# Down projection: the last six depth tiles move from plain products to seven-product quads in two token groups, with weights issued ahead of operands

## The chip, the cores and the metric

The kernel runs on one core of one Trainium2 chip. The metric is the time of one execution on the device in microseconds (us); for the kernel before it is the median of three runs. A profile of one further execution was taken and is what all rows below come from. Engines are named as the profile names them: PE (TensorE matmul), PEld (TensorE weight load), DVE (VectorE), ACT (ScalarE), POOL (GpSimd), SP (SyncE, whose queue, SPq, issues all transfers of this kernel).

## The reference, cut to what matters

One layer of a decoder step over 2048 prompt tokens and 64 sample tokens, width 1024:

```python
h = rms_norm(x, pre_mix_g)
z = h @ w_in                        # q, k, v, sg_u, sg_v, mq, gate_logits (3 x 1024)
attn = windowed_attention(q, k, v)  # 8 heads of 64
sg   = spatial_gating(gelu(sg_u), layer_norm(gelu(sg_v)))
memo = memory_attention(mq, mem_k, mem_v)
proj = einsum('blnc,ncd->blnd', stack([attn, sg, memo]), w_o)
mixed = sum(sigmoid(gate_logits) * proj, axis=branch)
x = x + rms_norm(mixed, post_mix_g)
up = rms_norm(x, pre_ffn_g) @ w_up               # 1024 -> 2 x 2816
gate, val = split(conv3(up) + conv_b)            # width-3 causal convolution
f = (gelu_tanh(gate) * val) @ w_down             # 2816 -> 1024
y = x + rms_norm(f, post_ffn_g)
```

The outputs are y, the new window keys and values, the memory keys and values, the normalised spatial-gating values of the samples and the last rows of `up`.

## The kernel before

All 2112 tokens are laid out with channels on the 128 partitions and tokens on the free axis. Products are done in float32 split into a high and a low part (`split`: ACT rounds to the high part, line 76, then DVE subtracts, line 77), and each product of 128 channels takes three matmuls (`PASSES`: high-high, high-low, low-high).

The work runs in these stages. `pass_a`: projections and both attentions. `pass_b`: spatial gating. `gate_phase`: the 3 x 1024 gate logits and their sigmoid. `mix_phase`: output projection, gating, sum, post norm. `up_phase`: the up projection with convolution and gelu, writing `act_d` to DRAM. `down_phase`: the down projection and the final norm.

From `gate_phase` on the tokens are taken in three groups of 704 (`T2`), each in two chunks of 352 (`CW`). Gate, up and most of down use a seven-product scheme (class `Strassen`): a block of two output tiles by two chunks, over eight depth tiles of 128 (two halves of `HK` = 4), takes seven products of 4 x 3 = 12 matmuls of 128x352, 84 instead of 96. The products need seven weight operands (three raw ones, `a11`, `a12`, `a22`, and four sums, `s1` to `s4`) and seven token operands (`b11`, `t1`, `b21`, `t2`, `b22`, `t3`, `t4`, each of four tiles). `operands` loads the tokens, forms differences on DVE (line 793) and splits each tile (28 splits, 16 differences). `weights` loads the raw parts (line 824) and splits them, and loads the sums ready made and already split from `sum_d` in DRAM (line 850). Each of the seven weight operands takes one tile of the pool `wo`, which has ten tiles in up and down.

The sums for up and down are made earlier by `prep_sums`: one call loads four blocks of 256 KB (line 108), forms four sums on DVE (line 113), splits each, and stores four tiles of 512 KB to `sum_d` (line 116). The calls for the 22 up tiles stand in `pass_b` (the first `NF1` = 14, two behind each of the first seven of nine token items) and in the gate jobs of groups 1 and 2 (eight); eight calls for down stand between jobs of `up_phase`, two in group 0, five in group 1, one in group 2. In `pass_b` they have a pool of two weight tiles and one of five raw tiles; the pools of `gate_phase` lie over these.

`down_phase` has, in each group, two blocks `b` of eight depth tiles, each four `quad`s of seven products (line 885 by way of `product`), whose results are added into eight sum tiles `ys` (lines 1235 on ACT and 1240 on DVE). The six remaining depth tiles (`ND`) go through `plain`: eight output tiles by two chunks, each 6 x 3 = 18 matmuls (line 1285), with operands from `load_acts`, an addition into `ys` (line 1293) and the squares for the final norm (lines 1295 to 1299). `load_acts` takes its tiles from the pools of `b22`, `t3` and `t4`. `final` (lines 1302 to 1320) scales and adds the residual and stores; for groups 0 and 1 it is written behind the first quad of the next group. The pool of sum tiles, `yd`, has ten.

The order on each engine is laid down when the kernel is built, by a planner with times of its own that takes what is ready by the order of the program text; `high_priority` moves a piece ahead. An engine runs its list in that order and waits at the head of it. In `jobs`, `operands` of a group stands ahead of `weights` of its first job.

In `mix_phase`, `post_mix` of one group runs among the matmuls of the next: for each of eight tiles DVE scales `m` in place (line 1004), POOL adds `x` in place (line 1007), the result is stored and squared. `ffn_phase` makes the pools of up and down; `up_phase` begins with `ops0`, the token operands of group 0, under `high_priority(None)`.

Of the kernel before, what the change touches and what calls it, by code (L numbers as in the profile page):

```python
# [15 lines left out]
P = 128  # L16
# [7 lines left out]
T2 = 704  # L24
# [10 lines left out]
NF1 = 14  # L35
# [8 lines left out]
def tile_decoder_layer(ctx, tc, I, O):  # L44
# [9 lines left out]
    sum_d = [dpool.tile([4, P, 2, 512], F32, tag=f"sumd{f}", name=f"sum_d{f}") for f in range(NF + 20)]  # L54
# [48 lines left out]
    def prep_sums(rw, wo, w, sums, nm):  # L103


        def block(i):
            t = rw.tile([P, 512], F32, tag="raw", name=f"r{i}_{nm}")
            nc.sync.dma_start(out=t, in_=w[:, i * 512 : (i + 1) * 512])
            return t

        def total(i, p, m, op):
            t = rw.tile([P, 512], F32, tag="raw", name=f"s{i}_{nm}")
            nc.vector.tensor_tensor(out=t, in0=p, in1=m, op=op)
            r = wo.tile([P, 2, 512], F32R, tag="w", name=f"ws{i}_{nm}")
            split(r[:, 0], r[:, 1], t)
            nc.sync.dma_start(out=sums[i], in_=_f(r))
# [632 lines left out]
def stage2(tc, I, O, br, rbc_d, x1_d, acx_d, act_d, sum_d, sg_d, gains, split, PASSES, rstd_rows, prep_sums, m_d, acm_d):  # L749
# [14 lines left out]
    class Strassen:  # L764
# [9 lines left out]
        def operands(self, xs, nm, gain, rb):  # L774
# [21 lines left out]
            J = range(HK)  # L796
# [6 lines left out]
            for j in J:  # L803
                load(j + HK)
                put("b21", j, chunk(x[j + HK], 0))
            for j in J:
                put("t2", j, sub(t[j], chunk(x[j + HK], 1), t[j]))
            for j in J:
                put("b22", j, chunk(x[j + HK], 1))
            for j in J:  # L810
                put("t3", j, sub(chunk(x[j], 1), chunk(x[j + HK], 1), chunk(x[j], 1)))
            for j in J:
                put("t4", j, sub(t[j], chunk(x[j + HK], 0), t[j]))
            return ops

        def weights(self, w, sums, first, nm):

            _, _, wo, rw, _, _ = self.pools
            raw = {}

            def block(i):
                if i not in raw:
                    raw[i] = rw.tile([P, HK * P], F32, tag="raw", name=f"r{i}_{nm}")
                    nc.sync.dma_start(out=raw[i], in_=w[:, i * 512 : (i + 1) * 512])
# [17 lines left out]
            for n, i in (("a11", 0), ("s1", 0), ("a12", 1), ("s2", 2), ("s4", 3), ("s3", 1), ("a22", 3)):  # L842
                t = wo.tile([P, 2, HK * P], F32R, tag="w", name=f"w{n}_{nm}")
                if n[0] == "a":
                    split(t[:, 0], t[:, 1], block(i))
                elif first:
                    split(t[:, 0], t[:, 1], total(i))
                    nc.sync.dma_start(out=sums[i], in_=_f(t))
                else:
                    nc.sync.dma_start(out=_f(t), in_=sums[i])  # L850
# [25 lines left out]
        def product(self, q, bank, w, o, start):  # L876
# [5 lines left out]
            ps, n = banks[bank], 0  # L882
            for j in range(HK):
                for a, b in PASSES:
                    nc.tensor.matmul(  # L885
                        ps[:, :CW], lhsT=ws[w][:, a, j], rhs=ops[o][j][:, b],
                        start=(start and n == 0), stop=(n == 3 * HK - 1), skip_group_check=True,
# [19 lines left out]
def gate_phase(c2, tc, env):  # L907
# [572 lines left out]
```

## Time and profile before

| | |
|---|---|
| time, median of 3 runs | 2978.36 us (2975.37 to 2981.42) |
| profiled execution, its own time | 2972.76 us |
| its span, first to last instruction | 2970.9 us |
| granted TensorE clock, mean | 0.984 |
| PE busy | 2868.4 us, 97% |
| DVE, ACT, POOL busy | 69%, 47%, 17% |
| HBM traffic over the span | 246 GB/s |

The span is 1.9 us short of the profiled execution's time, and that time is 5.6 us short of the median. In the tables of stretches the figures behind the length are the busy time of each engine in it, in the order PE, PEld, DVE, ACT, POOL, each with its count of instructions, then the granted clock (1.00 is 2.4 GHz), the share in which the DMA engines were busy, and GB/s. In the timelines a row is a start, a length, and what ran; in brackets stands the idle time ahead of it and what ended it. Neighbouring matmuls and vector instructions overlap a little in these rows, so a rate is read from start to start.

### The profile page before, as it was taken

What the parts mean: (1) busy time and instruction counts of PE and PEld (TensorE: products, weight loads), DVE (VectorE), ACT (ScalarE), POOL (GpSimd) and SP (SyncE); (2) the same over time, 40 slices, a digit from 0 to 9 for tenths busy, and PEclk for the clock granted to TensorE, in tenths of its full rate; (3) what the DMA queues carried; (4) which work ended last, traced back from release to release, by engine and by line L of the source; (5) the groups of instructions that cost most, each with busy time, mean ns of one, the idle gap of its engine ahead of it and who ended that gap; (6) DMA issues with size and microseconds to landing.
All of it is one profiled execution on the core that took longest, in us unless ns stands there. A gap on an engine that the chain in (4) does not pass through costs nothing.

```text
span 2970.9 us, 52583 instructions
## 1 busy us (share of the span) xinstructions
PE 2868.4 (97%) x19340; PEld 2821.0 (95%) x19340; DVE 2057.4 (69%) x3901; ACT 1395.8 (47%) x2793; POOL 499.2 (17%) x576
## 2 busy tenths in 40 slices
PE   8999999996999999999999999999999999999997
PEld 8998998996999999999989999999999999999997
DVE  6676567888767353468787777867785667767667
ACT  5555556334555354423325555555554454334333
POOL 3221100010000000035552211311242121000000
PEclk9999999998999999999999999999999999999998
DMA  6123223887889999867678987898787778576674
GB/s 213 52 68 88 73 69 115 266 294 269 326 309 350 340 358 342 319 222 247 207 270 297 336 327 245 309 335 328 241 321 244 242 241 287 198 271 230 210 268 134
DMA packets 310945, 732.32 MB, mean 247 GB/s; under 512 B 37968, under 2 KB 90192, under 8 KB 310672
## 3 DMA queue, kind: packets, MB, share of 16 engines
q1 hardware_dynamic: 310688, 728.97, 70.5%
q8 instruction: 153, 2.51, 0.3%
q14 instruction: 104, 0.85, 0.1%
HBM read 553.55 MB, written 176.27 MB: 246 GB/s over the span
## 4 chain that ended last, share of the span: by engine, by line
PE 87%; DVE 4%; DMA 4%; issue 2%; ACT 2%; POOL 1%; SPq 0%; DVEq 0%; ACTq 0%; POOLq 0%
PE ps_xu L885 17%; PE ps_xg L885 9%; PE ps_yu L885 9%; PE ps_p L1029 8%; PE ps_xd L885 6%; PE ps_yg L885 5%; PE ps_p L1285 5%; PE ps_wu L885 4%; PE ps_q L215 3%; PE ps_yd L885 3%; PE ps_mqp L229 3%; PE ps_wg L885 2%; PE ps_kv L215 2%; PE ps_sv L215 2%; PE ps_wd L885 1%
## 5 line engine op out<-in xcount | busy, mean ns | idle before, releaser
L1170 DVE SCALAR_TENSOR_TENSOR c<-e,k_conv_w,c 128x704 f32<-128x704 f32 (+1 forms) x264 | 252.0, 956 | 109.6 <-ACT c L1166 104.0
L1029 PE MATMUL ps_p<-b,w_p 128*128 128x352 f32 x1728 | 285.4, 327 | 11.7 <-DVE m L1038 9.0
L1029 PEld LDWEIGHTS ps_p<-b,w_p 128*128 128x128 f32 x1728 | 281.9, 191 | 13.1 <-issue 9.5
L885 PE MATMUL ps_xu<-ot_u,ws_u 128*128 128x352 f32 x1584 | 275.3, 323 | 0.0
L885 PEld LDWEIGHTS ps_xu<-ot_u,ws_u 128*128 128x128 f32 x1584 | 257.2, 188 | 0.0
L1042 POOL TENSOR_TENSOR m<-m,sl 128x704 f32<-128x704 f32 x48 | 105.4, 2204 | 653.4 <-DMA bx<-br 574.3
L77 DVE TENSOR_TENSOR wa_u<-r_u,wa_u 128x512 fp32r<-128x512 f32 x198 | 138.8, 704 | 24.4 <-ACT wa_u L76 22.0
L1166 ACT ACTIVATE c<-e,k_conv_b,k_conv_w 128x704 f32<-128x704 f32 (+1 forms) x132 | 129.6, 982 | 50.5 <-DVE e L1145 39.5
L885 PE MATMUL ps_xg<-ot_h,ws_g 128*128 128x352 f32 x864 | 152.0, 324 | 0.0
L76 ACT CAST wa_u<-r_u 128x512 fp32r<-128x512 f32 x198 | 123.1, 624 | 61.4 <-PE ps_yu L885 44.1
L885 PE MATMUL ps_xu<-ob_u,wa_u 128*128 128x352 f32 x792 | 149.0, 323 | 0.5 <-ACT sq_m L988 0.5
L1157 POOL COPY tails<-e 128x2 f32<-128x2 f32 x88 | 71.5, 813 | 456.5 <-DVE e L1145 446.4
L885 PE MATMUL ps_yu<-ot_u,ws_u 128*128 128x352 f32 x792 | 142.8, 325 | 3.9 <-DVE sl L1041 3.9
L885 PE MATMUL ps_wu<-ob_u,wa_u 128*128 128x352 f32 x792 | 146.6, 323 | 0.0
L885 PEld LDWEIGHTS ps_xg<-ot_h,ws_g 128*128 128x128 f32 x864 | 141.5, 188 | 0.2 <-ACT ws_g L76 0.2
L1285 PE MATMUL ps_p<-a,wd 128*128 128x352 f32 x864 | 140.3, 323 | 0.3 <-DVE y L1293 0.3
L1285 PEld LDWEIGHTS ps_p<-a,wd 128*128 128x128 f32 x864 | 138.4, 188 | 0.6 <-DVE y L1293 0.6
L885 PE MATMUL ps_xu<-ot_u,wa_u 128*128 128x352 f32 x792 | 138.2, 324 | 0.0
L885 PE MATMUL ps_yu<-ob_u,ws_u 128*128 128x352 f32 x792 | 137.8, 323 | 0.0
L885 PEld LDWEIGHTS ps_yu<-ot_u,ws_u 128*128 128x128 f32 x792 | 130.8, 190 | 4.2 <-DVE sl L1041 4.2
L885 PEld LDWEIGHTS ps_xu<-ob_u,wa_u 128*128 128x128 f32 x792 | 130.4, 189 | 0.8 <-ACT sq_m L988 0.8
L885 PEld LDWEIGHTS ps_wu<-ob_u,wa_u 128*128 128x128 f32 x792 | 130.3, 188 | 0.0
(381 smaller groups left out, 6690.6 us busy)
## 6 DMA issues: line engine op xcount, KB each, us to landing
ws_u<-sum_d SPq DMA_DIRECT2D x264, 512.0 KB, 5.5
r_u<-in_w_dram SPq DMA_DIRECT2D x286, 256.0 KB, 5.1
ws_g<-sum_d SPq DMA_DIRECT2D x96, 512.0 KB, 7.7
ws_d<-sum_d SPq DMA_DIRECT2D x96, 512.0 KB, 4.5
sum_d<-ws_u SPq DMA_DIRECT2D x88, 512.0 KB, 4.0
r_g<-in_wg_dram SPq DMA_DIRECT2D x120, 256.0 KB, 5.2
r_d<-in_w4s_dram SPq DMA_DIRECT2D x104, 256.0 KB, 4.1
sg_d<-sg SPq DMA_DIRECT2D x72, 352.0 KB, 5.0
```

The source lines that it names most:

```text
L76: nc.scalar.copy(out=hi, in_=src)
L77: nc.vector.tensor_tensor(out=lo, in0=src, in1=_f(hi), op=ALU.subtract)
L215: nc.tensor.matmul(ps[:nt, :256], lhsT=h[k // 4][:, a, k % 4, c0 : c0 + nt], rhs=wv[:, b, k], start=(n == 0), stop=(n == 3 * KT - 1),)
L229: nc.tensor.matmul(ps[:, :nt], lhsT=wv[:, a, k, half * P : (half + 1) * P], rhs=h[k // 4][:, b, k % 4, :nt], start=(n == 0), stop=(n == 3 ...
L885: nc.tensor.matmul(ps[:, :CW], lhsT=ws[w][:, a, j], rhs=ops[o][j][:, b], start=(start and n == 0), stop=(n == 3 * HK - 1), skip_group_chec ...
L1029: nc.tensor.matmul(ps[:, c, :CW], lhsT=w[:, a, 4 * oo + k], rhs=bs[k][:, b, c * CW : (c + 1) * CW], start=(i == 0), stop=(i == 11),)
L1042: nc.gpsimd.tensor_tensor(out=mx[o], in0=mx[o], in1=sg, op=ALU.add)
L1157: nc.gpsimd.tensor_copy(out=tails[:, ft], in_=e[:, T2 : T2 + 2])
L1166: nc.scalar.activation(c[:, :cwid], e[:, 2:ew], AF.Identity, bias=cb[:, ft : ft + 1], scale=cw[:, ft, 2:3])
L1170: nc.vector.scalar_tensor_tensor(out=c[:, :cwid], in0=e[:, t : t + cwid], scalar=cw[:, ft, t : t + 1], in1=c[:, :cwid], op0=ALU.mult, op1= ...
L1285: nc.tensor.matmul(ps[:, :CW], lhsT=w[k // 4][:, a, k % 4], rhs=acts[k][c][:, b], start=(n == 0), stop=(n == 3 * ND - 1),)
```

## The change

1. In groups 0 and 1 of `down_phase` the six depth tiles behind the first sixteen become a third block (`b` = 2) of four quads with `hk` = 3: seven products of nine matmuls, weights and sums 384 wide, from a new array `w4t` with the same numbers as the last part of `w4`. `squares` is called as each pair of sum tiles is complete. Group 2 keeps `plain` as it was.
2. Four more calls of `prep_sums`, 384 wide, make the sums for this block. The calls for down now stand in group 1 (five) and group 2 (seven) of `up_phase`.
3. `NF1` goes from 14 to 11: `pass_b` has three calls fewer. The gate jobs do tiles 11 to 18, and the tiles 19 to 21 are done in group 0 of `up_phase`, behind jobs 10, 13 and 16.
4. At the start of each group (gate, up) and each block (down), `weights` of the first job stands ahead of `operands`.
5. The pool of sum tiles has twelve tiles instead of ten, that of weight tiles nine instead of ten.
6. In `post_mix` DVE writes a tile `t` (one buffer) in place of `m`, and POOL adds `t` and `x` into `m`.
7. `ops0` stands under `high_priority(300)` instead of `high_priority(None)`.

```diff
-NF1 = 14
+NF1, NF2 = 11, 19
@@ operands / weights / product
-        def operands(self, xs, nm, gain, rb):
+        def operands(self, xs, nm, gain, rb, hk=HK):
-            J = range(HK)
+            J = range(hk)
...
-        def weights(self, w, sums, first, nm):
+        def weights(self, w, sums, first, nm, hk=HK):
-            raw = {}
+            raw, wide = {}, hk * P
...
-            ps, n = banks[bank], 0
-            for j in range(HK):
+            ps, n, hk = banks[bank], 0, len(ops[o])
+            for j in range(hk):
@@ gate_phase jobs
-        todo = list(range(NF1, NF))
+        todo = list(range(NF1, NF2))
+            ws = eng.weights(I["wg"][0], sum_d[NF], g == 0, f"g{g}_0")
             ops = eng.operands(lambda k: I["xT"][:, k, c0 : c0 + T2], f"h{g}", 0, rb)
             for i in range(12):
-                yield f"g{g}_{i}", eng.weights(I["wg"][i], sum_d[NF + i], g == 0, f"g{g}_{i}"), ops, Sink(g, i)
+                if i:
+                    ws = eng.weights(I["wg"][i], sum_d[NF + i], g == 0, f"g{g}_{i}")
+                yield f"g{g}_{i}", ws, ops, Sink(g, i)
@@ post_mix
+            t = xp.tile([P, T2], F32, tag="t", name=f"tm_{g}_{o}")
             nc.vector.scalar_tensor_tensor(
-                out=m, in0=m, scalar=gains[:, 2, o : o + 1], in1=rs, op0=ALU.mult, op1=ALU.mult
+                out=t, in0=m, scalar=gains[:, 2, o : o + 1], in1=rs, op0=ALU.mult, op1=ALU.mult
             )
-            nc.gpsimd.tensor_tensor(out=m, in0=m, in1=x, op=ALU.add)
+            nc.gpsimd.tensor_tensor(out=m, in0=t, in1=x, op=ALU.add)
@@ ffn_phase, up_phase
-        pool(c2, nm, n, "right") for nm, n in (("ldf", 1), ("rawf", 5), ("wof", 10))
+        pool(c2, nm, n, "right") for nm, n in (("ldf", 1), ("rawf", 5), ("wof", 9))
-    with tc.high_priority(None):
+    with tc.high_priority(300):
...
-        preps = [(g, f) for g, fs in ((0, (11, 14)), (1, (2, 5, 8, 11, 14)), (2, (2,))) for f in fs]
+        preps = [(g, f) for g, fs in ((1, (2, 5, 8, 11, 14)), (2, (1, 4, 7, 9, 11, 13, 15))) for f in fs]
...
+                    w = I["w4s"][i] if i < 8 else I["w4t"][i - 8]
+                    prep_sums(rw, wo, w, sum_d[NF + 12 + i], f"d{i}", 512 if i < 8 else 384)
+                if g == 0 and f in (10, 13, 16):
+                    u = NF2 + (f - 10) // 3
+                    prep_sums(rw, wo, I["w3"][u], sum_d[u], f"u{u}")
...
             if g + 1 < NG2:
+                ws = eng.weights(I["w3"][0], sum_d[0], False, f"u{g + 1}_0")
                 ops = eng.operands(lambda k: x1_d[g + 1][k], f"u{g + 1}", 3, rb)
@@ down_phase
-    yp, sp = pool(c2, "yd", 10), pool(c2, "sd", 1)
+    yp, sp = pool(c2, "yd", 12), pool(c2, "sd", 1)
...
+        done(0)
         add(1, 1, eng.product(q, "x", "s3", "t3", False))
-        return lambda: put(1, 0, eng.product(q, "x", "a22", "t4", False))
+        def last():
+            put(1, 0, eng.product(q, "x", "a22", "t4", False))
+            done(1)
+        return last
+    def squares(acc, y, o, c0, c1, nm):
+        if o == 0:
+            nc.scalar.activation(acc[:, c0:c1], y[:, c0:c1], AF.Square)
+        else:
+            sq = sp.tile([P, T2], F32, tag="sq", name=f"sq_{nm}")
+            nc.scalar.activation(sq[:, c0:c1], y[:, c0:c1], AF.Square)
+            nc.vector.tensor_tensor(out=acc[:, c0:c1], in0=acc[:, c0:c1], in1=sq[:, c0:c1], op=ALU.add)
...
-        for b in range(NB):
+        for b in range(NB + (g + 1 < NG2)):
+            hk = (HK, HK, ND // 2)[b]
+            ws = eng.weights(
+                I["w4s"][4 * b] if b < NB else I["w4t"][0], sum_d[NF + 12 + 4 * b], False, f"d{g}_{b}_0", hk
+            )
...
+                end = quad(nm, ws, ops, two, b == 0, end, *((done,) if b == NB else ()))
...
-        acts = load_acts(g)
         if g + 1 < NG2:
-            plain(g, acts, ys, (0, 1), acc, end)
-            held, end = (g, ys, acc, (0, 1)), None
+            held = g, ys, acc, (0, 1)
         else:
+            acts = load_acts(g)
             plain(g, acts, ys, (0,), acc, end)
```

## Rows read from the trace of the kernel before

**Rows 1.** The page: busy time, share of the span and instructions of each engine.

```profile
PE 2868.4 (97%) x19340; PEld 2821.0 (95%) x19340; DVE 2057.4 (69%) x3901; ACT 1395.8 (47%) x2793; POOL 499.2 (17%) x576
```

**Rows 2.** Stretches: busy time of PE, PEld, DVE, ACT, POOL, clock, DMA share, GB/s.

```profile
715.00:760.40 45.40, 17.03 (x72) 15.15 (x73) 42.76 (x80) 21.40 (x48) 0.00 (x0) 0.66 0.74 264
...
916.00:1081.00 165.00, 163.32 (x1012) 162.42 (x1010) 82.80 (x150) 76.71 (x159) 0.00 (x0) 1.00 0.92 345
...
1855.00:2153.00 298.00, 298.00 (x1874) 297.97 (x1873) 221.50 (x337) 161.42 (x289) 65.63 (x89) 1.00 0.86 304
2153.00:2452.00 299.00, 299.00 (x1868) 298.81 (x1867) 203.76 (x364) 158.07 (x280) 79.22 (x175) 1.00 0.77 262
...
2643.00:2657.00 14.00, 7.66 (x27) 6.91 (x26) 12.66 (x19) 3.27 (x7) 0.00 (x0) 0.67 0.63 199
2657.00:2783.00 126.00, 126.00 (x786) 126.00 (x785) 88.72 (x179) 54.06 (x115) 0.00 (x0) 1.00 0.68 235
```

**Rows 3.** Timeline of PE at the end of `pass_b` and the start of gate.

```profile
712.87 1.05 PE L735 MATMUL psg<-sgwb,vg 128*128 128x128 f32 x8
720.01 2.08 PE L735 MATMUL psg<-sgwb,vg 128*128 128x128 f32 x8 [6.09 <-DVE ob L739]
740.35 0.96 PE L885 MATMUL ps_xg<-ob_h,wa_g 128*128 128x352 f32 x2 [18.25 <-ACT wa_g L76]
```

**Rows 4.** Sums on DVE (line 113), and SP's queue, at the same place.

```profile
531.00:733.00 202.00, 37.25 (x56) 0.97 0.83 280
640.00:700.00 60.00, 12.63 (x19) 1.00 0.86 294
...
731.92 0.92 SPq L116 DMA_DIRECT2D sum_d<-ws_u  x2
...
735.96 1.37 SPq L824 DMA_DIRECT2D r_g<-in_wg_dram  x3
```

**Rows 5.** Timelines of DVE: start-to-start times, one row of each kind.

```profile
737.63 1.84 DVE L77 TENSOR_TENSOR ot_h<-x_h,ot_h 128x352 fp32r<-128x352 f32 x4
...
731.21 1.29 DVE L77 TENSOR_TENSOR ws_u<-s_u,ws_u 128x512 fp32r<-128x512 f32 x2
```

**Rows 6.** Timeline of PE: one run of matmuls of `plain`.

```profile
2574.12 40.96 PE L1285 MATMUL ps_p<-a,wd 128*128 128x352 f32 x255
```

**Rows 7.** Timelines of PE, DVE and ACT behind the first change of group in down.

```profile
2643.04 0.49 PE L885 MATMUL ps_xd<-ob_d,wa_d 128*128 128x352 f32 x2
2648.84 3.31 PE L885 MATMUL ps_xd<-ob_d,wa_d 128*128 128x352 f32 x10 [5.32 <-DVE wa_d L77]
...
2641.20 6.99 DVE L1315 SCALAR_TENSOR_TENSOR y<-y,c_gains,rs_d 128x704 f32<-128x704 f32 x8
2648.70 3.30 DVE L1319 TENSOR_TENSOR y<-y,xf 128x704 f32<-128x704 f32 x4
...
2652.67 0.45 ACT L1235 COPY y<-ps_xd 128x352 f32<-128x352 f32 x1 [0.88 <-DMA out_yT_dram<-y]
```

**Rows 8.** Timelines in mix, groups 0 to 1: DVE, PE, POOL.

```profile
1366.86 12.78 DVE L1004 SCALAR_TENSOR_TENSOR m<-m,c_gains,rs 128x704 f32<-128x704 f32 x8
...
1380.59 19.63 PE L1029 MATMUL ps_p<-b,w_p 128*128 128x352 f32 x108 [4.52 <-DVE m L1038]
...
1367.89 4.69 POOL L1007 TENSOR_TENSOR m<-m,xr 128x704 f32<-128x704 f32 x2 [6.18 <-DVE m L1004]
1374.14 4.75 POOL L1007 TENSOR_TENSOR m<-m,xr 128x704 f32<-128x704 f32 x2 [1.56 <-DMA xr<-in_xT_dram]
```

**Rows 9.** One line each, all uses: DVE scaling and POOL addition in `post_mix`.

```profile
L1004 DVE SCALAR_TENSOR_TENSOR m<-m,c_gains,rs x16: 939/1656/2415, 1366.9 to 1479.3; 128x704 f32<-128x704 f32 x16
...
L1007 POOL TENSOR_TENSOR m<-m,xr x16: 1697/2354/2707, 1367.9 to 1510.9; 128x704 f32<-128x704 f32 x16
```

**Rows 10.** Waits of PE from 1500 to 1560 us: total, times, longest.

```profile
PE ps_yu L885 <- DVE sl L1041: 3.9, 1, 3.9
```

**Rows 11.** DMA issues by tile: count, size, median us to landing.

```profile
ws_u<-sum_d SPq DMA_DIRECT2D x264, 512.0 KB, 5.5
```

More of the change, by code (lines that the diff above doesn't have):

```diff
@@ L53, in tile_decoder_layer @@
     acx_d = [dpool.tile([P, T2], F32, tag=f"acxd{g}", name=f"acx_d{g}") for g in range(NG2)]
-    sum_d = [dpool.tile([4, P, 2, 512], F32, tag=f"sumd{f}", name=f"sum_d{f}") for f in range(NF + 20)]
+    sum_d = [dpool.tile([4, P, 2, 512], F32, tag=f"sumd{f}", name=f"sum_d{f}") for f in range(NF + 24)]
     sg_d = [dpool.tile([P, NTOK], F32, tag=f"sgd{i}", name=f"sg_d{i}") for i in range(24)]
@@ L101, in rstd_rows, with prep_sums @@
         return r, (i_mean, i_pow)
[L103 removed]
+    def prep_sums(rw, wo, w, sums, nm, wide=512):
         def block(i):
             t = rw.tile([P, 512], F32, tag="raw", name=f"r{i}_{nm}")
[L108 to L109 removed]
+            nc.sync.dma_start(out=t[:, :wide], in_=w[:, i * wide : (i + 1) * wide])
+            return t[:, :wide]
         def total(i, p, m, op):
[L112 removed]
+            t = rw.tile([P, 512], F32, tag="raw", name=f"s{i}_{nm}")[:, :wide]
             nc.vector.tensor_tensor(out=t, in0=p, in1=m, op=op)
[L114 removed]
+            r = wo.tile([P, 2, 512], F32R, tag="w", name=f"ws{i}_{nm}")[:, :, :wide]
             split(r[:, 0], r[:, 1], t)
[L116 removed]
+            nc.sync.dma_start(out=sums[i][:, :, :wide], in_=_f(r))
             return t
@@ L847, in weights @@
                     split(t[:, 0], t[:, 1], total(i))
-                    nc.sync.dma_start(out=sums[i], in_=_f(t))
+                    nc.sync.dma_start(out=sums[i][:, :, :wide], in_=_f(t))
                 else:
-                    nc.sync.dma_start(out=_f(t), in_=sums[i])
+                    nc.sync.dma_start(out=_f(t), in_=sums[i][:, :, :wide])
                 ws[n] = t.rearrange("p s (k c) -> p s k c", c=P)
@@ L1225, in down_phase, with quad @@
     op_, wo, rw, lp = (env[n] for n in ("op_", "wo", "rw", "lp"))
-    yp, sp = pool(c2, "yd", 10), pool(c2, "sd", 1)
+    yp, sp = pool(c2, "yd", 12), pool(c2, "sd", 1)
     eng = Strassen(ps2, op_, wo, rw, None, lp)
-    def quad(nm, ws, ops, ys, first, end):
+    def quad(nm, ws, ops, ys, first, end, done=lambda o: None):
         q = [nm, ws, ops, None, {}]
@@ L1329, in down_phase, with done @@
                     ys += [yp.tile([P, T2], F32, tag="y", name=f"y_{g}_{2 * op + h}") for h in range(2)]
-                i, nm = 4 * b + op, f"d{g}_{b}_{op}"
-                ws = eng.weights(I["w4s"][i], sum_d[NF + 12 + i], False, nm)
-                end = quad(nm, ws, ops, ys[2 * op : 2 * op + 2], b == 0, end)
+                i, nm, two = 4 * b + op, f"d{g}_{b}_{op}", ys[2 * op : 2 * op + 2]
+                if op:
+                    ws = eng.weights(I["w4s"][i] if b < NB else I["w4t"][op], sum_d[NF + 12 + i], False, nm, hk)
+                def done(o, op=op, two=two, acc=acc, nm=nm):
+                    squares(acc, two[o], 2 * op + o, 0, T2, f"{nm}_{o}")
+                end = quad(nm, ws, ops, two, b == 0, end, *((done,) if b == NB else ()))
                 if held:
@@ L1420, in _layout @@
     )
+    r["w4t"] = np.stack(
+        [
+            np.concatenate([dn[2 * op + oo][:, 16:].reshape(P, (NF - 16) * P) for oo in range(2)], 1)
+            for op in range(4)
+        ]
+    )
     r["w4"] = np.stack([dn[o][:, 16:].reshape(P, (NF - 16) * P) for o in range(KT)])
```

39 lines of the change are left out of this document (19 added, 20 removed).

## The prediction

> **What bounds the kernel now.** I read the shares by engine first: PE is busy 97% of the span, DVE 69%, ACT 47% [rows 1]. So the time is PE's work and the roughly 100 us in which PE stands (span less busy time). Then I went through the stretches: the two later groups of up, 298 and 299 us long, have no idle PE at all [rows 2]. The reader is to see that an edit there can gain nothing and can only lose cover. Then I looked at the stretches in which PE is not full, and in each at the timelines of PE, of the engine that it waits for, and of that engine's own supplier. Three places matter. From the end of `pass_b` to the start of gate, 715 to 760.4 us, PE has 17 us of busy records, at a mean clock of 0.66 [rows 2]; it waits 6.09 us and then 18.25 us in one piece [rows 3]. Behind each of the two changes of group in down there is a stretch such as 2643 to 2657 us, with 7.66 us busy and a clock of 0.67 [rows 2], opened by a wait of 5.32 us [rows 7]. In mix PE waits 4.52 us behind each of two changes of group [rows 8]. The rest is spread out or belongs to the tail, which the change leaves as it is.
>
> **Fewer matmuls.** One matmul takes 0.16 us, as 255 take 40.96 us [rows 6]. `plain` has 8 x 2 x 18 = 288 of them in a group, the new quads 4 x 7 x 9 = 252. Two groups save 72, and 72 x 0.16 = 11.5 us. This is certain as long as PE stays the bound there.
>
> **The opening of gate.** In the 45.4 us from 715 to 760.4 there are 64 matmuls of 352 columns (72 less the eight of line 735), worth 10.2 us, and about 1 us of the others; 34 us are lost. What is late is the first raw gate weight: SP issues it at 735.96 us, only after the last `sum_d` stores of `prep_sums` at 731.92 us [rows 4], because the gate's raw pool lies over that of `prep_sums`. These calls form 56 sums from 531 to 733 us, the last part of them 19 in 60 us, 3.2 us for a sum [rows 4]. Three calls fewer are 12 sums, or 38 us, so the chain should end near 695 us, before `pass_b`'s last long matmuls end at 713 us [rows 3]. The raw weights can then be there when PE is free, and the wait of 6.09 us, for a DVE that holds sums ahead of line 739, should shrink with them. Not all of the 34 us comes back: part of the token operands lies over tiles that `pass_b` uses to its end, and the splits left then are some 7 for weights at 0.60 us and 16 plus 12 token instructions at 0.44 us on DVE [rows 5], 16.5 us against 13.4 us for the first job's 84 matmuls, with latencies between. I leave 10 us lost and take 24 back; the bounds are 2 (the operands come out as late as now) and 32. The order of weights and operands alone is put at nothing beyond this: if PE does not lack weights at a change of group, as in the up stretches without idle, the cover is there already.
>
> **The moved sums.** A call is eight DVE instructions of 0.60 us, 4.8 us, eight DMAs and four slots of the weight pool. Group 0 of up gets three calls in place of two; group 2 gets three full ones and four narrow ones in place of one, 2 x 4.8 + 4 x 3.7 = 24 us of DVE (384 wide taken at 0.46 us, between the rows for 352 and 512). That makes 204 + 24 = 228 us of 299, 76%, where group 1 now has 221 of 298 without an idle PE [rows 2]. The bytes, 2 x 3.1 + 4 x 2.4 = 16 MB more in 299 us, bring 262 to about 315 GB/s; gate runs at 345 [rows 2]. They queue on SP between the weight loads of the jobs, whose covers are next. A weight tile freed by one product is needed nine products later instead of ten; that leaves 8 x 1.93 = 15 us for a load that lands in 5.5 us [rows 11]. With the four slots of a call in the rotation it is about 4 x 1.93 = 8 us, for a load that can be queued behind waiting ones. I take 2 us in all, between 0 and 15.
>
> **The changes of group in down.** From 2643 to 2657 us there are 27 matmuls, 4.3 us of work, so 9.7 us are lost, and the pattern stands twice. At the front of the chain is `final`: its eight scalings hold DVE from 2641.20 to 2648.2 us, ahead of the low half of a weight, and a little later ACT can only fill a sum tile once the old one is stored (2652.67 us) [rows 7]. With ten sum tiles only the first quad of a group has free ones; PE goes on with products that need none and then stands. Twelve tiles cover one more quad, 84 x 0.16 = 13.4 us, more than the loss. Part of the loss is clock: behind the wait ten matmuls take 3.31 us in place of 1.6 [rows 7].
>
> What speaks against this part is DVE. The third block asks of DVE, in 252 x 0.16 = 40.5 us of PE: 28 additions at 0.44 us, 12 low halves of weights at 0.46, seven square sums at 0.80, 21 splits and 12 differences at 0.44: 12.3 + 5.5 + 5.6 + 14.5 = 38 us, 94% (0.44 from [rows 5], 0.80 from four in 3.30 us [rows 7]). `plain` asks 16 x 0.44 + 8 x (0.60 + 0.34) + 5.6 + 12 x 0.44 = 25 us in 46 us. And because `plain` leaves the pools of `b11` and `t1` alone, part of the next group's splits is done under it now; with the third block all seven pools are in use to its last quad. So next to be late is the next group's operands, 44 x 0.44 = 19 us, and behind them `final`, 8 x (0.87 + 0.80) = 13 us. Until the third quad of the new group begins, 10 + 27 us of PE work, DVE has these 32 us and some 14 us of additions and weights. I take 4 us lost at each change instead of 9.7, a gain of 11 us, and 2 us lost at each start of a third block, 4 us. Bounds for both together: from a gain of 19 us to a loss of 20.
>
> **Mix.** Eight scalings run in one piece of 12.78 us [rows 8], the median one 1.66 us against 0.94 at the fastest [rows 9], and the product behind them is late for PE. With one buffer `t`, a scaling waits for POOL's addition before it, median 2.35 us [rows 9], so the planner must lay other DVE work between them. That should bring the product forward. But what stands behind a waiting scaling on DVE then waits for POOL and for POOL's load of `x`. I take 4 us of the 9 back, between 9 back and 27 lost (below). The Trainium skill (SBUF — State Buffer, SBUF: two separate sides) gives DVE and POOL a shared port that one of them holds alone for a whole instruction when DVE reads two tensors. By that rule eight scalings and the four additions in that piece would take 8 x 0.94 + 9.4 = 16.9 us; the measured 12.78 us differs and decides, though POOL's lengths are rough. If the rule held in full, laying scalings and additions apart would free no DVE time, mix would give 0 and the sum would be 2938 us.
>
> **Start of up.** PE waits 3.9 us for a product that DVE does late [rows 10], while `ops0` is moved ahead. A lower priority can serve that product earlier and the operands later. No row separates them: nothing, between 4 gained and 10 lost.
>
> **The sum.** 11.5 + 24 + 11 - 4 + 4 - 2 = 44.5 us less than 2972.8, thus 2928. The profiled execution lies 5.6 us below the median of the runs; put against that median, the prediction is 2934 us.
>
> **Rivals.**
>
> A, the case above, 0.50. Own range 2918 to 2950.
>
> B, gate opens hardly earlier, 0.15: the planner keeps the token operands where they are, or the operand pools come free only with `pass_b`'s last tiles. For it: DVE is busy 43 of the 45 us [rows 2]. Against it: the raw weights come behind the last store [rows 4]. Then 4 us come back instead of 24: 2954. In this form the change does not do what its smaller `NF1` suggests.
>
> C, DVE becomes the bound around the third block, 0.12. For it: the 94% above; against it: 70% in 2657 to 2783 us [rows 2]. If each change of group and third block loses 12 us more than I put: 2958. The Trainium skill (PSUM — Partial Sum Buffer, Engine vs sequencer instructions) has DVE's queue strictly in order; the trace agrees, as a weight's low half stood 5.32 us behind eight scalings [rows 7], and by that rule the 32 us of operands and `final` hold up every later product's addition, which is this case.
>
> D, mix is serialised by `t`, 0.08: eight scalings and additions one behind the other are 8 x (0.94 + 2.35) = 26 us in place of 12.8, 13.5 us more of a blocked DVE in each of two groups, and no gain: 2934 + 27 + 4 = 2965.
>
> E, slower, 0.07: nine weight tiles no longer cover up. It has 66 jobs and 15 calls for sums; below 44.5 / 66 = 0.67 us a job the kernel stays ahead, above it loses. If the two jobs around each call lose a product's time, 1.93 us, that is 58 us, and with the clock falling in such waits more: 2934 + 58 = 2992 or above. Against it: no job in up waits now.
>
> F, better, 0.08: gate loses only 2 us, the changes of group nothing, mix gives 9: 2934 - 8 - 8 - 5 = 2913.
>
> **How the numbers follow.** The time is A's, 2934. From 2908 to 2968 lie A, B, C, D and F but for their tails; E and those tails, about 0.15, are outside. A measurement of this kernel tells some 0.2% (6 us) from no change. A, B, C and F lie on the faster side of 2972.4, D mostly; with the tails of C and D, where losses meet, that is 0.88 faster, 0.04 the same, 0.08 slower.
>
> **What would show it.** Right: in the profile after, the first gate matmul at 715 to 725 us and the last `sum_d` store of `pass_b` near 695; 72 matmuls fewer; up without idle PE; waits of under 5 us where the groups of down change; no wait on line 1038's counterpart above 3 us. Wrong: a wait of some 20 us at the opening of gate (B), DVE above 90% with waits of PE on sums or token splits from the third block on (C), DVE waiting for POOL's addition in mix (D), or PE in up waiting for weight loads (E).

## The result, and the profile after

The kernel after takes 2944.7 us (median of four runs, 2939.8 to 2946.3) against 2977.0 us (four runs, 2975.4 to 2981.4): a ratio of 0.9887, 95% interval 0.9869 to 0.9904. The forecast was 2934 us, with a range from 2908 to 2968. The profiled execution took 2939.84 us, its span 2938.0 us: 32.9 us less than before by span, where the sum said 44.5.

The page of the kernel after, busy time, share and instructions by engine; 19268 against 19340 matmuls [rows 1] is the forecast 72 fewer:

```profile
PE 2859.3 (97%) x19268; PEld 2807.0 (96%) x19268; DVE 2091.0 (71%) x3991; ACT 1408.1 (48%) x2819; POOL 505.9 (17%) x576
```

Where the time went, by the first matmul of each stage on PE's timeline (`psg` at the end of `pass_b`, `ps_p` for mix, `ps_xu` for up, `ps_xd` for down):

| stage | before, us | after, us | difference | predicted |
|---|---|---|---|---|
| end of `pass_b` and gate | 535.9 | 510.1 | -25.8 | -24 |
| mix | 304.4 | 296.2 | -8.1 | -4 |
| up | 899.7 | 913.8 | +14.1 | +2 |
| down | 518.0 | 505.4 | -12.6 | -18.5 |

The rest, 0.4 us, lies ahead of `psg`. So gate and mix gave more than the sum had put there, up lost 14 us where 2 had been put, and down gave two thirds.

**Gate opens on time.** PE's timeline and SP's queue of the kernel after, at the place of [rows 3] and [rows 4]:

```profile
712.48 1.05 PE L735 MATMUL psg<-sgwb,vg 128*128 128x128 f32 x8
714.32 1.16 PE L735 MATMUL psg<-sgwb,vg 128*128 128x128 f32 x8 [0.79 <-DVE ob L739]
717.12 0.42 PE L885 MATMUL ps_xg<-ob_h,wa_g 128*128 128x352 f32 x1 [1.65 <-ACT ob_h L76]
...
686.66 5.22 SPq L116 DMA_DIRECT2D sum_d<-ws_u  x3
692.16 0.79 SPq L742 DMA_DIRECT2D br<-ob  x1
693.00 1.57 SPq L824 DMA_DIRECT2D r_g<-in_wg_dram  x3
```

The last stores of sums are issued by 691.9 us in place of 731.92, the first raw gate weight at 693.0 in place of 735.96, and the first gate matmul runs at 717.1 us, within the forecast 715 to 725, in place of 740.35; the waits of 6.09 and 18.25 us are 0.79 and 1.65.

**Stretches of the kernel after**, columns as in [rows 2]: the opening of gate, the start of up, 303 us from just ahead of up's group 2 on, the two changes of group in down, the two third blocks.

```profile
712.48:760.00 47.52, 41.47 (x235) 39.12 (x234) 46.43 (x86) 32.06 (x69) 0.00 (x0) 0.93 0.76 271
1518.86:1558.86 40.00, 32.52 (x193) 31.97 (x192) 36.06 (x60) 23.66 (x48) 7.78 (x11) 0.91 0.60 211
...
2117.00:2420.00 303.00, 298.82 (x1834) 295.91 (x1833) 224.23 (x399) 164.26 (x295) 89.94 (x167) 0.99 0.86 306
...
2632.00:2650.00 18.00, 10.75 (x50) 10.17 (x49) 18.00 (x31) 5.42 (x13) 0.00 (x0) 0.72 0.66 246
2793.00:2809.00 16.00, 11.24 (x57) 10.46 (x56) 16.00 (x28) 6.48 (x15) 0.00 (x0) 0.89 0.73 256
...
2548.00:2590.00 42.00, 42.00 (x264) 42.00 (x263) 37.42 (x79) 19.11 (x40) 0.00 (x0) 1.00 0.89 286
2710.00:2752.00 42.00, 42.00 (x264) 42.00 (x263) 36.61 (x79) 19.44 (x41) 0.00 (x0) 1.00 0.93 290
```

Read with 0.16 us a matmul [rows 6]. The opening of gate holds 219 matmuls of line 885 (235 less 16 of line 735), 35.0 us, and 2.2 us of line 735: 10.3 of 47.5 us are lost, where 10 were left. The third blocks run without idle PE, with DVE at 89 and 87%: the 94% that was feared did not decide. But the changes of group still lose 18 - 8.0 = 10.0 and 16 - 9.1 = 6.9 us, and up is no longer full. Two places in up show it: the 303 us of group 2, below, and the start. The kernel before has in the 40 us from its first product of up

```profile
1553.16:1593.16 40.00, 36.06 (x217) 35.63 (x218) 32.72 (x52) 23.24 (x46) 11.63 (x14) 0.96 0.80 299
```

217 matmuls where the kernel after has 193, which is 3.8 us.

**The change of group in down.** PE, DVE and ACT behind the first change, at the place of [rows 7]:

```profile
2590.76 2.08 PE L885 MATMUL ps_yd<-ot_d,ws_d 128*128 128x352 f32 x12
...
2601.65 1.61 PE L885 MATMUL ps_xd<-ot_d,wa_d 128*128 128x352 f32 x9
...
2612.41 0.71 PE L88 MATMUL ps_sd<-ones,acc 128*88 128x1 f32 x8
...
2617.38 1.02 PE L98 MATMUL ps_sd<-ident,rstd_d 88*128 88x88 f32 x8
...
2622.44 0.72 PE L88 MATMUL ps_sd<-ones,acc 128*88 128x1 f32 x8
...
2627.43 1.02 PE L98 MATMUL ps_sd<-ident,rstd_d 88*128 88x88 f32 x8
...
2641.29 3.89 PE L885 MATMUL ps_xd<-ot_d,ws_d 128*128 128x352 f32 x12 [6.39 <-ACT y L1246]
...
2609.72 0.89 DVE L1275 TENSOR_TENSOR acc<-acc,sq_d 128x704 f32<-128x704 f32 x1
...
2623.27 0.16 DVE L92 TENSOR_SCALAR rstd_d<-ps_sd 88x4 f32<-88x4 f32 x1 [3.91 <-PE ps_sd L88]
...
2629.05 6.99 DVE L1335 SCALAR_TENSOR_TENSOR y<-y,c_gains,rs_d 128x704 f32<-128x704 f32 x8
...
2640.78 0.45 ACT L1246 COPY y<-ps_xd 128x352 f32<-128x352 f32 x1 [6.15 <-DMA out_yT_dram<-y]
```

Follow it backwards. PE waits 6.39 us for ACT's copy into a sum tile; the copy starts 6.15 us late, when the tile's old content has been stored; the store waited for an addition that DVE does behind eight scalings in one piece of 7 us, from 2629.05; these waited for the norm, which goes through PE four times, at places in PE's queue some 5 us apart; the norm waited for the last square sum at 2609.72. The first two rows, the new group's second product and the old group's last one, are used further down. The waits of [rows 7] on a weight's low half are gone, and the wait for a stored sum tile, of which they showed 0.88 us, has taken their place.

**The start of up's group 2.** PE, and SP's queue ahead of it:

```profile
2156.58 2.19 PE L885 MATMUL ps_xu<-ot_u,wa_u 128*128 128x352 f32 x12 [0.54 <-ACT u_u L894]
2160.41 0.59 PE L885 MATMUL ps_xu<-ob_u,wa_u 128*128 128x352 f32 x2 [1.64 <-ACT wa_u L76]
...
2163.25 3.30 PE L885 MATMUL ps_xu<-ob_u,wa_u 128*128 128x352 f32 x10 [1.07 <-DVE wa_u L77]
...
2119.52 0.33 SPq L824 DMA_DIRECT2D r_u<-in_w_dram  x1
...
2143.27 0.33 SPq L108 DMA_DIRECT2D r_d<-in_w4s_dram  x1
...
2151.79 0.33 SPq L108 DMA_DIRECT2D r_d<-in_w4s_dram  x1
...
2153.61 0.39 SPq L824 DMA_DIRECT2D r_u<-in_w_dram  x1
```

From 2119.5 to 2153.6 us no raw weight of up is issued. Four raw tiles of a call for sums (`r_d`, two of them shown) go out in between and are held while DVE is busy with the new group's operands; the raw weights behind them come when PE already needs them.

### The profile page after: what moved, and what is told of

It is laid out like the page before. It is cut to its first block, busy times and chain, and to the rows that moved or that the text cites. A ratio compares the mean times of both kernels' runs of the same rounds, so it can differ in the third digit from the quotient of the medians.

```text
span 2938.0 us, 52740 instructions
## 1 busy us (share of the span) xinstructions
PE 2859.3 (97%) x19268; PEld 2807.0 (96%) x19268; DVE 2091.0 (71%) x3991; ACT 1408.1 (48%) x2819; POOL 505.9 (17%) x576
## 5 line engine op out<-in xcount | busy, mean ns | idle before, releaser
L1046 POOL TENSOR_TENSOR m<-m,sl 128x704 f32<-128x704 f32 x48 | 96.7, 2020 | 631.9 <-DMA sl<-sg_d 553.5
L1161 POOL COPY tails<-e 128x2 f32<-128x2 f32 x88 | 89.0, 1012 | 462.0 <-DVE e L1149 440.5
L885 PE MATMUL ps_xu<-ob_u,wa_u 128*128 128x352 f32 x792 | 151.1, 326 | 2.9 <-ACT wa_u L76 1.6
L885 PE MATMUL ps_xd<-ot_d,ws_d 128*128 128x352 f32 x720 | 131.1, 330 | 9.8 <-ACT y L1246 9.8
L885 PEld LDWEIGHTS ps_xd<-ot_d,ws_d 128*128 128x128 f32 x720 | 120.8, 193 | 10.5 <-ACT y L1246 10.5
```

Of the source, the lines that this page charges most:

```text
L885: nc.tensor.matmul(ps[:, :CW], lhsT=ws[w][:, a, j], rhs=ops[o][j][:, b], start=(start and n == 0), stop=(n == 3 * hk - 1), skip_group_chec ...
L1046: nc.gpsimd.tensor_tensor(out=mx[o], in0=mx[o], in1=sg, op=ALU.add)
L1161: nc.gpsimd.tensor_copy(out=tails[:, ft], in_=e[:, T2 : T2 + 2])
```

## The experiments

All ratios are to the kernel before on the same chip, with 95% intervals; stage times are from each run's profile, as in the table. In down the "period" is the time from the norm's first matmul (`ps_sd`) at the first change of group to that at the second, one whole group. Its matmuls are 960 x 0.16 = 153.6 us with `plain`, 924 x 0.16 = 147.8 us with the third block; what is above that, 13.8 us before and 13.0 after, is lost or (some 3.5 us) the norm's own matmuls.

Each stage time comes from one execution. Over runs whose edits lie in other stages it repeats within 1.5 us in gate (510.1 to 511.7), 1.4 us in up (912.8 to 914.2) and 3.8 us in mix (294.4 to 298.2); smaller differences say nothing.

### Where up lost: place of the calls, or nine weight tiles

```diff
-        preps = [... (2, (1, 4, 7, 9, 11, 13, 15))]
+        preps = [... (2, (3, 5, 7, 9, 11, 13, 15))]
```

> The kernel after, with the calls for sums behind jobs 1 and 4 of group 2 of up moved to jobs 3 and 5. Theory 1: what up lost at the start of its group 2 (four waits from 2156.6 to 2163.3 us, then ten matmuls in 3.30 us) comes from the call behind job 1, which holds raw tiles while the new group's operands fill DVE, so that the raw weights of the next jobs are issued late. Then those waits go, up takes about 906 us in place of 913.8, and the whole is about 8 us below the kernel after. Theory 2, nine weight tiles are too few: the waits stay wherever the calls stand, and up stays within 2 us of 913.8.

Measured: 2944.4 us, 0.9897 (0.9881 to 0.9913), up 913.3 us. The waits at 2156 to 2163 us are gone, but up gained nothing: a wait of 2.41 us appears at 2239 and one of 1.23 us at 2367 us. Theory 1 has the cause of these four waits and not the gain. Theory 2 has the number, up within 2 us of 913.8, and not the waits: nothing waits at the old place. With the seven calls two jobs apart other waits appear, and whether the weight tiles are behind them is for the next run to say.

```diff
-        ... (("ldf", 1), ("rawf", 5), ("wof", 9))
+        ... (("ldf", 1), ("rawf", 5), ("wof", 10))
-    yp, sp = pool(c2, "yd", 12), pool(c2, "sd", 1)
+    yp, sp = pool(c2, "yd", 10), pool(c2, "sd", 1)
```

> The kernel after, with ten weight tiles in place of nine and ten sum tiles in place of twelve. Up tells of the weight tiles: by theory 2 (nine are too few) up falls from 913.8 to 905 us or less, its waits of the start of group 2 gone; by theory 1 (the place of the call) it stays within 2 us. Down tells of the sum tiles: by the prediction's account (each pair of tiles covers one quad, 13.4 us) the waits at the changes of group come one quad earlier and cost 8 to 10 us each more than now; by its rival (the wait is for a norm that is late by its own chain, which then starts earlier too) down stays within 3 us of 505.4.

Measured: 2954.9 us, 0.9938 (0.9917 to 0.9958); up 913.7 us, down 520.0 us. The stretch 2117 to 2420 us with ten weight tiles:

```profile
2117.00:2420.00 303.00, 298.54 (x1846) 295.11 (x1845) 223.41 (x401) 165.56 (x297) 91.35 (x169) 1.00 0.87 309
```

It has 298.5 us of PE, as with nine (298.8), and 12 matmuls more, 1.9 us, which the rest of up gives back. The weight tiles are not what up lacks. For down, see below.

```diff
-        preps = [... ((1, (2, 5, 8, 11, 14)), (2, (1, 4, 7, 9, 11, 13, 15)))]
+        preps = [... ((1, (2, 5, 8, 11, 14, 17)), (2, (3, 6, 9, 12, 15, 18)))]
```

> The kernel after, with the twelve calls for down's sums as six behind jobs 2, 5, 8, 11, 14 and 17 of group 1 and six behind jobs 3, 6, 9, 12, 15 and 18 of group 2 of up, in place of five and seven. Theory: the loss of some 8 us in group 2 is the price of seven calls that stand two or three jobs apart, one of them beside the new operands; three jobs apart and clear of the operands they cost nothing, as the five of group 1 do, and up takes 906 to 908 us in place of 913.8. Rival: each call beyond the five costs a piece of PE wherever it stands; up stays within 2 us of 913.8.

Measured: 2938.9 us, 0.9875 (0.9859 to 0.9891), up 903.9 and down 512.8 us. No wait over 1 us is left in groups 1 and 2 of up. Part of the 9.9 us is only a boundary, since down's first product now runs earlier among up's last ones and down then waits 3.61 us at 2456.8; by itself this run does not separate theory and rival. The last run of the next section does.

### The wait for a sum tile in down

```diff
-            rstd_rows(chunk(acc, c), CW, ...)   # for each chunk c, then its copy
+            rstd_rows(acc[:, c0:c1], c1 - c0, ...)   # once; a bank and a copy for each chunk
```

> The kernel after, with the sums of squares of both chunks summed over the partitions and raised to the power in one step in the last norm of down, in place of one chunk after the other. Theory: the waits of 6.39 and 3.39 us at the changes of group stand at the end of a chain of four small matmul groups, each at its place in PE's queue some 5 us behind the one before, from the last square sum at 2610.6 to the first scaling at 2629.1 us. With one step less the first scaling comes some 5 to 8 us earlier, the waits fall below 1 us, and group 1 and 2 of down together take 8 to 12 us less. Rival: the stored sum tiles wait for DVE behind the operands of the new group, and nothing is gained (within 2 us).

Measured: 2934.5 us, 0.9862 (0.9845 to 0.9879); down 497.2 us, 8.2 us less; period 153.8 us in place of 160.8. PE and DVE behind the first change of group:

```profile
2610.70 1.34 PE L88 MATMUL ps_sd<-ones,acc 128*88 128x1 f32 x16
...
2621.67 1.02 PE L98 MATMUL ps_sd<-ident,rstd_d 88*128 88x88 f32 x8
...
2634.72 2.19 PE L885 MATMUL ps_xd<-ot_d,ws_d 128*128 128x352 f32 x12 [0.64 <-ACT y L1246]
...
2623.77 6.99 DVE L1346 SCALAR_TENSOR_TENSOR y<-y,c_gains,rs_d 128x704 f32<-128x704 f32 x8
```

Both sums go through PE in one turn of 16, so there are three turns in place of four. From the last square sum to the scalings it is 16.1 us (2607.66 to 2623.77) in place of 19.3, and the wait is 0.64 in place of 6.39 us; at the second change the longest is 1.65 in place of 3.39. The rival, DVE's operands, falls: nothing was taken from them.

```diff
-    yp, sp = pool(c2, "yd", 12), ...
+    yp, sp = pool(c2, "yd", 14), ...
-                x = sp.tile([P, T2], F32, tag="x", ..., bufs=4)
+                x = sp.tile([P, T2], F32, tag="x", ..., bufs=2)
```

> The kernel after, with fourteen sum tiles in place of twelve and two tiles in place of four for the input that the last norm adds. By the prediction's account (a pair of tiles covers one quad, 13.4 us) the waits at the changes of group, 6.39 and 3.39 us with half clock behind them, are gone, and groups 1 and 2 of down take 10 to 14 us less. Rival: with more tiles the planner lets the norm slip by a quad again, as it did from ten to twelve, and the waits only move: within 3 us of now.

Measured: 2925.5 us, 0.9836 (0.9818 to 0.9855); down 489.9 us, 15.5 us less; period 152.8 us. The norm did not slip: the scalings start 38.3 us behind the second product, as in the kernel after. The longest wait at a change is 1.05 us, and behind so short a wait twelve matmuls take 2.19 us in place of 3.89; the granted clock over 2632 to 2650 us is 1.00 in place of 0.72:

```profile
2637.77 2.19 PE L885 MATMUL ps_xd<-ot_d,ws_d 128*128 128x352 f32 x12 [1.05 <-ACT y L1246]
...
2632.00:2650.00 18.00, 16.95 (x106) 16.65 (x105) 18.00 (x37) 12.95 (x30) 0.00 (x0) 1.00 0.93 329
```

The run with ten sum tiles is the other side of this: its waits at the changes are 11.5 us each,

```profile
2635.76 3.89 PE L885 MATMUL ps_xd<-ot_d,ws_d 128*128 128x352 f32 x12 [11.48 <-ACT y L1246]
```

and down takes 520.0 us, 2 us more than before, although the 72 matmuls are gone. So a pair of sum tiles is worth 14.6 us from ten to twelve and 15.5 us from twelve to fourteen. Both are differences of the whole of down, with two changes of group in it, so 7 to 8 us at each, where the prediction's account has a pair cover 13.4 us at each and the expectation for ten tiles had 8 to 10. From twelve to fourteen the waits left to win were smaller than a quad. From ten to twelve they were not, and the rows of the first change say what became of the rest: with twelve tiles PE comes to the wait 10.6 us later (2634.90 us in place of 2624.28), but the wait also ends 5.5 us later (2641.29 in place of 2635.76). With ten tiles PE is already idle while the norm runs, and from its first turn to the scalings it takes 13.3 us; with twelve PE's queue is still full, and it takes 16.6 us.

```diff
+ both edits above: yd 14, xf bufs=2, and one rstd_rows for both chunks
```

> The kernel after with fourteen sum tiles and the one-step norm together, which alone brought 15.5 and 8.2 us in down. Theory: both pay for the same wait for a stored sum tile, of which fourteen tiles leave 1.05 us at each change; together they bring no more than 2 us beyond the fourteen tiles, with down at 488 to 490 us. Rival: they add up, and down falls to about 482 us.

Measured: 2923.7 us, 0.9828 (0.9814 to 0.9843); down 487.3 us, period 151.1 us, no wait over 1 us at the changes. That is 2.6 us less in down than with fourteen tiles alone, a little over the theory's 2 and far from the 8.2 of a sum: in the main they pay for the same wait.

```diff
+ the same, and preps ((1, (2, 5, 8, 11, 14, 17)), (2, (3, 6, 9, 12, 15, 18)))
```

> Fourteen sum tiles, the one-step norm and the calls six and six. Theory: the calls' part is in up alone, so that the whole is 5 to 8 us below the run with fourteen tiles and the norm. Rival: with the last calls at jobs 15 and 18 they meet the first operands of down, and what up gains is lost at the start of down.

Measured: 2914.2 us, 0.9797 (0.9782 to 0.9811), 9.5 us below the run before it on the same chip, more than the 5 to 8 expected; by the spans of the two profiled executions it is 5.2 us (up 8.4 less, mix 2.3 and down 1.2 more). The stretch 2117 to 2420 us now:

```profile
2117.00:2420.00 303.00, 303.00 (x1894) 303.00 (x1894) 229.93 (x409) 168.77 (x307) 81.52 (x174) 1.00 0.85 304
```

PE is full with 60 matmuls more than in the kernel after, 9.6 us, at the same nine weight tiles and the same twelve calls in all, six of them in this group in place of seven. Group 1, with six in place of five, is as full as in the kernel after: 1661 against 1663 matmuls in 264 us of it. The theory holds: six calls in a group, three jobs apart and clear of the operands, are free. The rival's loss at the start of down is not there beyond 1.2 us (488.5 against 487.3). This is the fastest version that ran.

### The parts alone

```diff
 # kernel before
-    ("wof", 10)  ...  pool(c2, "yd", 10)
+    ("wof", 9)   ...  pool(c2, "yd", 12)
```

> The kernel before, with nine weight tiles and twelve sum tiles and nothing else. Theory 1, the prediction's: the tiles cover a quad, so that the waits of 5.32 us at both changes of group go and down falls from 518.0 to 500 to 508 us; nine weight tiles cost up less than 2 us with its eight calls, and the whole is 10 to 17 us faster. Theory 2: the waits at the changes are DVE's eight scalings ahead of a weight, whatever tiles there are; down stays within 3 us, and nine weight tiles cost up several us.

Measured: 2959.5 us, 0.9950 (0.9935 to 0.9964); down 500.1 us, up 902.7 us, period 158.4 us. Theory 1 holds: with `plain` kept, twelve tiles take the waits of 5.32 us away. The longest left behind the two changes are

```profile
2663.42 2.21 PE L885 MATMUL ps_xd<-ot_d,ws_d 128*128 128x352 f32 x12 [1.25 <-ACT y L1235]
...
2821.09 2.19 PE L885 MATMUL ps_xd<-ot_d,ws_d 128*128 128x352 f32 x12 [0.57 <-ACT y L1235]
```

And down is 5.3 us, and the period 2.4 us, shorter than in the kernel after: with twelve tiles the third block lost more at the changes than its 72 matmuls gave back. Up reads 3.0 us longer with nine weight tiles, over the theory's 2; but gate, which this run leaves as it was, reads 2.6 us longer too, so that a cost of nine tiles is not shown. The edit changes both pools, and the part of the sum tiles in down is not separated from that of the weight tiles.

```diff
 # kernel before
+NF1, NF2 = 11, 19
+                if g == 0 and f in (10, 13, 16):   # up: prep_sums of tiles 19 to 21
+        preps: (1, (2, 5, 8, 11, 14)), (2, (2, 6, 10))
```

> The kernel before, with one part of the change: eleven in place of fourteen calls for sums in pass_b, three of up's own calls behind jobs 10, 13 and 16 of its group 0, and the eight calls for down behind five jobs of group 1 and three of group 2. Theory: this alone opens the gate early; psg to mix falls from 535.9 to between 510 and 516 us, the whole by 20 to 25 us. Rival: it needs the weights ahead of the operands as well; then psg to mix stays above 522 us. Up, with ten weight tiles and few calls in group 2, stays within 4 us of 899.7 either way.

Measured: 2958.0 us, 0.9937 (0.9921 to 0.9952); end of `pass_b` and gate 512.7 us, up 902.0 us. The theory holds: 23.2 of the 25.8 us come with the moved sums alone. The whole gains 19 us and not 20 to 25, because down opens worse (526.4 us, a wait of 4.70 us at 2467); why it does was not tried.

```diff
-            ws = eng.weights(<first job>)      # gate, up, down
             ops = eng.operands(...)
+            ws = eng.weights(<first job>)
```

> The kernel after, with each group's operands ahead of its first weights again, in gate, up and down. Theory, as in the prediction: the order by itself is worth nothing, the gate's 25.8 us come from the sums that were moved; psg to mix stays within 3 us of 510.1, and the whole within 6 us of the kernel after. Rival: without it the raw weights queue behind 16 operand loads on SP, and the first gate matmul comes 5 to 12 us later; the changes of group in up and down lose too.

Measured: 2951.3 us, 0.9914 (0.9899 to 0.9928); end of `pass_b` and gate 513.8, up 913.9, down 512.8 us. The first gate matmul comes 5.8 us behind the first `psg` in place of 4.6, so the gate's gain is from the sums, with 3.6 us of it from the order: a little more than the theory's 3, and the whole is 6.6 us above the kernel after where the theory had 6. The rival's 5 to 12 us for the first matmul are not there. Down takes 7.4 us more, with a wait of 4.56 us at 2471 us. As much was lost there in runs that kept the order (512.8 us with later calls and with the calls six and six), so what of it is the order's stays open.

```diff
-                out=t, in0=m, ...   # then POOL: in0=t
+                out=m, in0=m, ...   # then POOL: in0=m
```

> The kernel after, with the scalings of the mix norm written in place again, without the tile t. Theory: mix's 8.1 us are those of the two waits of 4.5 us behind eight scalings in one piece, and t takes them away; without t mix takes about 304 us in place of 296.2. Rival: mix runs better because the gate ahead of it ends otherwise; it stays within 2 us of 296.2.

Measured: 2949.9 us, 0.9905 (0.9886 to 0.9924); mix 302.9 us. The two waits on the scalings in one piece are back:

```profile
1355.31 0.93 PE L1032 MATMUL ps_p<-b,w_p 128*128 128x352 f32 x2 [4.52 <-DVE m L1041]
...
1457.63 1.81 PE L1032 MATMUL ps_p<-b,w_p 128*128 128x352 f32 x5 [4.50 <-DVE m L1041]
```

So 6.7 of mix's 8.1 us are `t`, give or take the 3.8 us by which mix varies.

```diff
-    with tc.high_priority(300):
+    with tc.high_priority(None):
```

> The kernel after, with the first operands of up put ahead of all other work again, as in the kernel before. Theory: of up's loss about 4 us lie at its start (a wait of 6.58 in place of 3.93 us, with half clock behind it) and come from the lower priority, by which the last product of mix stands behind late operands; they come back, up takes about 910 us in place of 913.8. Rival: the start is set by the order of the last mix products on DVE whatever the priority; up stays within 1.5 us.

Measured: 2945.0 us, 0.9894 (0.9880 to 0.9909); up 908.4 us, mix 302.2 us. Up gets 5.4 us back, and mix gives 5.9: the operands of up taken early stand ahead of mix's last products, and PE waits 4.06 us there. The loss is moved, not saved. The end of gate reads 4.2 us longer in this profile (514.3 us), which the argument does not explain; the median is that of the kernel after.

## Why the prediction was right, and where its sum was wrong

The direction and the case were A: gate opens with the sums that were moved, the changes of group lose less, up stays nearly full. The time lies inside A's own range, 10.7 us above its 2934. That it came so near is in part luck: gate and mix gave 5.9 us more than the sum had, and so hid a third of the 18.0 us by which up and down fell short. Two of the signs named for being right did not come: up is not without idle PE, and one of the waits at the changes of group is over 5 us. Step by step:

**Fewer matmuls**, -11.5 us: 72 fewer, as counted. **The opening of gate**, -24: measured -25.8, of which 23.2 come with the moved sums alone; 10.3 us are still lost where 10 were left. The order of weights and operands, put at nothing, is worth 3.6 us of it. **Mix**, -4: measured -8.1, 6.7 of them shown to be `t`. The term was set at half of its upper bound, and the upper bound was nearer. Rival D's order was there in a mild form: the scalings stand apart, DVE waits for POOL ahead of eight of them, 8.2 us in all, and nothing that PE needs stood behind one for long (PE's longest wait in mix is 1.84 us).

**The moved sums and nine weight tiles**, +2 between 0 and 15: measured +14.1 for up, of which some 9.6 us lie in group 2 and 3.8 at the start. This is the first mis-sized term. The working asked whether a landed weight tile is free in time and found the cover; ten tiles in place of nine changed nothing in the kernel after, and in the kernel before no cost of nine is shown. What it did not ask was where a call stands beside the new operands, and how close one call follows the other: seven calls two or three jobs apart, the first behind job 1, took 9.6 us of PE in 303 us; six calls three jobs apart, the first behind job 3, take none. DVE was at 74% in that stretch (224.2 of 303) and at 76% in the one that runs full (229.9): its share does not tell the two apart. Whether the spacing or the seventh call costs more was not separated: with seven calls two jobs apart and clear of the operands the loss stayed. Rival E was there in small: raw weights come late beside a call, and the price was some 10 us and not 58. **Start of up**, 0 between -4 and +10: the wait is 6.58 in place of 3.9 us [rows 10]; the run with the old priority shows it is an exchange with mix.

**The changes of group in down**, -11: measured 10.0 and 6.9 us lost in place of twice 9.7, a gain of 2.5 us. This is the second. The account "two tiles cover one quad, 13.4 us" had the direction and not the size: a pair is worth 14.6 and 15.5 us over both changes, 7 to 8 at each. What the step left out is that the third block moves the norm. The new group's second product, the last square sum and, with ten tiles, the scalings, in the kernel before and in the run with the third block and ten sum tiles:

```profile
2616.84 2.08 PE L885 MATMUL ps_yd<-ot_d,ws_d 128*128 128x352 f32 x12
...
2619.33 0.89 DVE L1299 TENSOR_TENSOR acc<-acc,sq 128x704 f32<-128x704 f32 x1
...
2590.80 2.08 PE L885 MATMUL ps_yd<-ot_d,ws_d 128*128 128x352 f32 x12
...
2608.79 0.88 DVE L1275 TENSOR_TENSOR acc<-acc,sq_d 128x704 f32<-128x704 f32 x1
...
2624.88 6.99 DVE L1335 SCALAR_TENSOR_TENSOR y<-y,c_gains,rs_d 128x704 f32<-128x704 f32 x8
```

Before, the last square sum comes 2.5 us behind the new group's second product and the scalings, at 2641.20 us [rows 7], 24.4 us behind it. In the kernel after they come 19.0 and 38.3 us behind it (2590.76, 2609.72 and 2629.05 us). A quad's last product is placed behind the next quad's first, and here it runs at 2601.65 us, 10.9 us behind the new group's second; its addition, its square and the norm's four turns through PE follow from there. With ten sum tiles and the third block the last square sum is 18.0 us behind as well, so that it is the third block that moves it and not the two tiles. The 13.9 us by which the scalings came later are about the quad that two tiles were to buy. With `plain`, whose last sums come at the end of the old group, twelve tiles leave 4.8 us of the period lost; with the third block 13.0; with the third block and fourteen tiles 4.9, with the norm in one step 6.0, with both 3.3. **Third blocks**, +4: measured nothing lost. The matmuls and the changes make a gain of 14.0 us and down shows 12.6; the 1.4 us between are not placed. Nor does the prediction speak of the opening of down: the two runs that only move calls in up have a wait of 3.6 us there, which the kernel after has not, and take 512.8 us. Rival C, DVE as the bound, fell: DVE was busy 18.00 of 18 us at the first change in the kernel after, and it is so with fourteen tiles too, where PE does 106 matmuls in the same 18 us in place of 50. (The 5.32 us that the rival gives for the low half behind eight scalings are PE's wait; the scalings take 6.99 us [rows 7].)

The prediction had "`final`" in its list of what comes next on DVE, 13 us of work. It asked how long it takes, not when it can start.

## What to carry to other kernels

Count extra buffers from the moment at which the old one is given back, not from the length of one step: an edit that defers the last product of a group defers the norm and the store behind it, and eats the buffers bought for it. Where PE goes through a short serial chain (sum, power, broadcast, copy) while its queue is full, every turn costs a queue place, here some 5 us; one turn less was worth 8.2 us, half of what two more tiles brought. Side work in a full stretch can be free or not at the same busy share: spread it evenly and clear of a change of operands before you give it more tiles. What each of the two is worth, and what one call less, was not separated here.

## What the runs showed of the hardware that was not expected

At the start of up DVE's instructions of one kind take 0.51 us, and some 2.0 us beside a POOL addition; the kernel after, DVE and POOL:

```profile
1520.85 0.51 DVE L793 TENSOR_TENSOR x_u<-x_u,x_u 128x352 f32<-128x352 f32 x1
1521.29 0.87 DVE L1045 TENSOR_TENSOR sl<-sl,ps_p 128x704 f32<-128x704 f32 x1
...
1522.52 2.00 DVE L793 TENSOR_TENSOR x_u<-x_u,x_u 128x352 f32<-128x352 f32 x1
...
1522.24 1.89 POOL L1046 TENSOR_TENSOR m<-m,sl 128x704 f32<-128x704 f32 x1 [1.69 <-DVE sl L1045]
```

The subtraction that starts at 1522.52 ends at 1524.52, 0.39 us behind the end of POOL's addition at 1524.13, much as if it had begun only there. Two more DVE instructions there end 0.38 us behind a POOL addition (at 1518.97 and 1520.93 us, POOL's at 1518.59 and 1520.55). That agrees with the rule that the prediction weighed in mix, the Trainium skill (SBUF — State Buffer, SBUF: two separate sides): one of the two holds the shared port for a whole instruction when DVE reads two SBUF tensors. In mix the 12.78 us of [rows 8] did not fit it; here the rows do, and no run was made to settle the difference. One row hints at it: the POOL addition that ends at 1518.59 us is recorded from 1514.91 on, 3.68 us, while DVE goes through four instructions of 0.51 us beside it, from 1515.19 to 1517.01 us. If that record holds a wait of POOL's own, the 9.4 us that the prediction took for POOL's four additions are too many.
